# Dealing the tokens into even and odd halves in a one-core decoder trunk

## The chip, the core and the metric

The kernel runs on one core of a Trainium2 chip. The core has a matrix engine (TensorE, PE in the profile, with PEld for its weight loads), VectorE (DVE), ScalarE (ACT), GpSimd (POOL) and SyncE (SP), which work on tiles in an on-chip memory of 128 partitions (SBUF) and on accumulators (PSUM). Each engine runs its own queue in order. ScalarE and SyncE also issue DMA transfers from their queues. The metric is the device time of one execution, in microseconds.

## What is computed

A decoder trunk for 256 tokens, width 2048, in fp32. First keys and values of 256 memory tokens for both layers; then a layer of gated linear attention (GLA, 4 heads, chunks of 64 tokens), a gated feed-forward, a layer of forgetting attention (12 heads), a second feed-forward and a closing norm. Each attention layer also has 4 heads that attend to the memory. Cut to what matters:

```
mem_n = rmsnorm(mem, norm_mem)
for i in range(2):
    if i == 1:                                 # shared keys, values and forget gates
        hs = rmsnorm(x, g_kv)
        fk, fv, fl = split_cols(hs @ w_kv, [1536, 1536, 12])
        fc = cumsum(log_sigmoid(fl + b_f))     # over tokens
    mk, mv = split_cols(mem_n @ mem_w_kv[i], [512, 512])
    h = rmsnorm(x, norm_mix[i])
    if i == 0:                                 # GLA
        q, k, v, glr, og, mq = split_cols(h @ w_in, [1024, 1024, 1536, 16, 1536, 512])
        g = log_sigmoid(glr @ w_gate_up + b_gate) / 16
        # S_t = diag(exp g_t) S_{t-1} + k_t v_t^T ;  o_t = q_t S_t   (chunks of 64)
        o = headwise_rmsnorm(gla(q / 16, k, v, g)) * gn_gain * silu(og)
    else:                                      # forgetting attention, causal
        q, mq = split_cols(h @ w_in, [1536, 512])
        o = softmax(q k^T / sqrt(128) + fc[t] - fc[s]) fv
    m = softmax(mq mk^T / sqrt(128)) mv
    x = x + concat(o, m) @ w_out
    u = causal_conv3(rmsnorm(x, norm_ffn[i]) @ w_up)      # 2 x 5632 wide, over tokens
    x = x + (silu(u[:, :5632]) * u[:, 5632:]) @ w_down
return rmsnorm(x, norm_final)
```

## The kernel before

All weights are streamed from HBM in fp32, in **units** of two 128-row chunks by up to 512 columns (512 KB, tile `raw`, issued by SyncE). A panel of a projection is 8 units (16 chunks). Every weight is used in two parts: ScalarE casts the high part (`whi`, line 207), VectorE subtracts it from the weight (`wlo`, line 216), and PE does 12 matmuls of a unit: high part of the activation by high weight (228), low part of the activation by high weight (229), high part of the activation by low weight (232), for both halves of the tokens. `raw` has 4 tiles, `whi` and `wlo` 3 each, so ScalarE can be some units ahead of PE. Activations are kept as `bufA` and `bufB`, 16 tiles each of features by 256 tokens with a high and a low part (`A`, `B` in the profile); `split` (lines 343 to 347) makes the two parts, one operation on ScalarE and one on VectorE for each tile.

A panel leaves PSUM with tokens on the partitions, two accumulators of 128 tokens by 512 columns. What needs features on the partitions is turned: ScalarE scales it (`scaled`), VectorE transposes it in blocks of 32 by 32 (`square`), one DMA writes the square to DRAM and four DMAs read it back, one for each block of 128 features. These five DMAs are issued by ScalarE's queue, between the casts. The class `Turn` does this with runs of 32 tokens (128 bytes) in the reads:

```
self.rows = dp.tile([2, 4, 32, 4, 4, 32], F32, name=tag, tag=tag, bufs=bufs)
nc.scalar.dma_start(dst(k).rearrange("p (n t) -> p n t", t=32),                  # read, L301
                    self.rows[:, :, :, :, k, :].rearrange("b q i r t -> (i r) (b q) t"))
```

It serves the memory keys, the queries and keys of GLA (`qk`), the keys `fkt`, the queries and gates (`back<-turned`), and the residual `x` after each layer (`xturned`), which is split with a gain into the next projection's input (346, 347). The feed-forward has a form of its own (lines 876 to 889): it interleaves the two token halves in the square, so that its reads have 64 tokens (256 bytes) in a run. For that its scale has to be in the interleaved order too, which `mixed` makes with a product of ones and a diagonal (`row`, line 411) and two reductions (425).

Values (`mv`, `gv`, `fvt`) stay with tokens on the partitions and are only scaled (line 778 for `fvt`).

Steps that follow a panel are registered with `later((n, step), ...)` and released after the cast of the n-th unit from then on: the write at 3, the four reads at 6, and then the work on what was read, from 8 on. In GLA the gates of a head are released at 7 and its whole core, the levels of the chunked attention (lines 635 to 686), at 9. Four memory heads or four fox heads come at 8, 9, 10 and 11. The tile scheduler orders every engine's queue from a simulated timeline, in program order as the priority, with the weight loads moved up.

After the last heads comes the output projection (`add_out`), whose last two units in two panels wait for the last tiles of `mix`; after it `then` turns the new `x`, block by block, for the next projection.

Of the kernel before, what the change touches and what calls it, by code (L numbers as in the profile page):

```python
# [130 lines left out]
M_PICK = M_LVL + NVER * len(LEVELS)  # L131
M_FOX = M_PICK + 2 * T
# [4 lines left out]
def _trunk(ctx: ExitStack, tc: tile.TileContext, xt, xtok, memt, wp, wgu, gns, gfin, cnv, par, msk, out):  # L137
# [14 lines left out]
    mask = const.tile([P, M_PICK], F32, name="mask")  # L152
# [116 lines left out]
    def turned(pool, bank, width, col):  # L269

        t = pool.tile([P, T], F32, name="narrow", tag="tmp", bufs=5)
        nc.gpsimd.memset(t, 0.0)

        def take(b, a):
            S.activation(t[:, b * P : b * P + width], a, AF.Copy, scale=col[:, b : b + 1])

        def turn():
            for b in range(2):
                bs = slice(b * P, (b + 1) * P)
                TE.transpose(bank[:, bs], t[:, bs], ident)  # L280
            return bank[:, :T]

        return take, turn

    class Turn:


        def __init__(self, tag="turned", bufs=4):
            self.square = tp.tile([P, 2, 16, 32], F32, name="square", tag="square", bufs=2)
            self.rows = dp.tile([2, 4, 32, 4, 4, 32], F32, name=tag, tag=tag, bufs=bufs)  # L290

        def put(self, b, src):
            V.transpose(self.square[:, b], src.rearrange("p (c t) -> p c t", t=32))  # L293

        def write(self):
            nc.scalar.dma_start(self.rows.rearrange("b q i r k t -> (q i) b (r k t)"),
                                self.square.rearrange("p b c t -> p b (c t)"))

        def read(self, dst, blocks=range(4)):
            for k in blocks:  # L300
                nc.scalar.dma_start(dst(k).rearrange("p (n t) -> p n t", t=32),  # L301
                                    self.rows[:, :, :, :, k, :].rearrange("b q i r t -> (i r) (b q) t"))

    def back():
        return tp.tile([P, 4, T], F32, name="back", tag="back", bufs=2)

    def to_features(scales, dst, *steps):
# [3 lines left out]
        def evac(b, a):  # L311
# [12 lines left out]
            if b:  # L324
                got = []

                def read():
                    t = dst()
                    got.append(t)
                    held[0].read(t if callable(t) else lambda k: t[:, k, :])  # L330

                later((3, held[0].write), (6, read), *[(n, lambda step=step: step(got[0])) for n, step in steps])
# [3 lines left out]
    def split(dst, i, src, g=None, dealt=False):  # L336
# [12 lines left out]
    class Norm:  # L349


        def __init__(self, n, tag="x"):
            self.n, self.tag = n, tag
            self.acc = self.y = self.r = self.m = None
# [61 lines left out]

        def mixed(self, picks):

            if self.m is None:
                row = self.row()  # L420
                self.m = sm.tile([P, 2], F32, name="mixed", tag="mixed")
                for h in range(2):
                    pick = picks[:, h * T : (h + 1) * T]
                    sq = sm.tile([P, T], F32, name="sq", tag="sq", bufs=2)
                    V.tensor_tensor_reduce(sq, row, pick, 1.0, 0.0, ALU.mult, ALU.max, self.m[:, h : h + 1])  # L425
            return self.m
# [56 lines left out]
    with tc.tile_pool(name="load", bufs=1) as lp:  # L483
# [3 lines left out]
        def take_mem(g, half):  # L487
# [10 lines left out]
            for i in range(2 * half, 2 * half + 2):  # L498
                k = 4 * g + i
                split(bufA, k, mt[g][:, i, :], mraw[0][:, k : k + 1])  # L500
# [4 lines left out]
        def keys(l):  # L505
            def scaled(got):
                for f in range(MEM_H):
                    V.tensor_tensor(mk[0][:, f, :], mk[0][:, f, :], nrm.row(), ALU.mult)
# [6 lines left out]
        def mv_out(l):  # L515
            return lambda b, a: S.activation(mv[l][:, b, :], a, AF.Copy, scale=nrm.col()[:, b : b + 1])
# [13 lines left out]
        with tc.issue_after(loads[-1].ins):  # L530
# [3 lines left out]
            nc.sync.dma_start(mask[:, M_SCAN:], msk[:, M_SCAN:M_PICK])  # L534
        proj_tm(("mv", 0), bufA, mv_out(0))
        for i in range(KC):
            split(bufB, i, xf[i], gain("mix0", i))
# [10 lines left out]
    def gla(nx, then):  # L548
        h, mix = bufB, bufA
        with tc.tile_pool(name="gla", bufs=1) as gp:  # L550
# [13 lines left out]
            def first_values(b, a):  # L564
                S.activation(v0[:, b, :], a[:, :DV], AF.Copy, scale=nx.col()[:, b : b + 1])
                take(b, a[:, DV:])
# [3 lines left out]
            proj_tm(("gv", 0), h, first_values)  # L570
# [21 lines left out]
            def core(hd, q, k, v, bc):  # L592
# [41 lines left out]
                for li, B in enumerate(LEVELS):  # L634
                    H = B // 4
# [28 lines left out]
                    for i, (o, w) in enumerate(VERSIONS):  # L664
                        o4 = a3.rearrange("p b (n t) -> p b n t", t=B)[:, :, :, (i + 1) * H :]
                        for g in range(2):
# [5 lines left out]
                                              p3[gs, :, o : o + w].rearrange("p b (n t) -> p b n t", t=(3 - i) * H))  # L672
                nrm = Norm(DV, "o")
                os = []
                for j in range(3):
# [7 lines left out]
                    os.append(o)  # L683
                for j, o in enumerate(os):
# [4 lines left out]
            def take_og(j):  # L689
                def gated(c):  # L690
                    def step(g):
                        for k in (c, c + 1):
# [3 lines left out]
                            V.tensor_tensor(o, *(mix[i][:, n, :].bitcast(F32) for n in range(2)), ALU.add)  # L696
# [5 lines left out]
                proj_tm(("og", j), h, to_features([(0, 4, nx.col)], back, (8, gated(0)), (9, gated(2))))  # L702

            for hd in range(GLA_H):
                v = values(hd) if hd else v0
                if hd:
                    proj_tm(("gv", hd), h, lambda b, a: S.activation(
                        v[:, b, :], a, AF.Copy, scale=nx.col()[:, b : b + 1]))
                bc = []
                def qk():  # L710
# [5 lines left out]
                    (7, lambda t, hd=hd, bc=bc: bc.append(gates(hd))),  # L716
                    (9, lambda t, hd=hd, v=v, bc=bc: core(hd, t[:, :2, :], t[:, 2:, :], v, bc[0]))))
            for j in range(3):
# [3 lines left out]
                *[(8 + c, lambda q, c=c: mem_attention(gp, 0, q[:, c, :], c, mix)) for c in range(4)]))  # L722
# [3 lines left out]
    def fox(nx, kept, then):  # L726
        hk, hq, mix = bufB, bufA, bufB
        with tc.tile_pool(name="fox", bufs=1) as fp:
# [11 lines left out]
            def queries(f):  # L740
                got = []

                def read():
# [312 lines left out]
```

## Time and profile before

| quantity | value |
|---|---|
| time, median of 3 runs | 2272.53 us (2269.84 to 2276.99) |
| the profiled execution | 2272.12 us, span 2270.3 us |
| granted TensorE clock, mean | 0.998 |
| moved by DMA | 509.09 MB, mean 224 GB/s |
| first layer's memory and GLA stages | 0 to 430 us |
| first output projection, x turned | 430 to 515 us |
| first feed-forward | 515 to 1100 us |
| its last down projection, keys and values of fox | 1100 to 1300 us |
| fox attention, output projection, x turned | 1300 to 1550 us |
| second feed-forward | 1550 to 2200 us |
| its end, closing norm | 2200 to 2270.3 us |

A line of a timeline has the start, the duration, the engine, the source line, the operation and, in brackets, how long the engine was idle before and what released it. A line of a group ends with its busy time, the mean of one in ns, and the idle time before them. A line of waits has the engine's instruction, what it waited for, the total in us, the count and the longest.

### The profile page before, as it was taken

To read this page: it belongs to the slowest core of one execution; us is meant where nothing else is said; L and a number is where in the kernel's file an instruction comes from. 1 tells how busy PE (TensorE), PEld (TensorE's weight loads), DVE (VectorE), ACT (ScalarE), POOL (GpSimd) and SP (SyncE) were. 2 spreads that over 40 slices of the span, in tenths; PEclk is the share of its full clock that TensorE was granted. 3 is DMA by queue.
4 is the path that set the end of the run, shared out by engine and by line. 5 is a ranking of instruction groups with operands and counts; after the bars stand their busy time and mean duration, and the time that the engine had idled before them with its cause. 6 is when DMAs were issued, how large, how long until landed. Compare 5 with 4: busy or idle time off the path is not lost.

```text
span 2270.3 us, 29243 instructions
## 1 busy us (share of the span) xinstructions
PE 2246.3 (99%) x10340; PEld 1875.3 (83%) x10340; DVE 1499.7 (66%) x2329; ACT 1239.8 (55%) x1852; POOL 2.9 (0%) x15
## 2 busy tenths in 40 slices
PE   9999999999999999999999999999999999999998
PEld 7888887888888888888878898877888888888886
DVE  7568987667665577656766546656776566755766
ACT  7555565546553565445555545555655355644654
POOL 0000000000000000000000000000000000000000
PEclk9999999999999999999999999999999999999999
DMA  9765567677775777657778966677876577766774
GB/s 316 244 203 169 191 211 218 196 238 253 243 230 193 230 241 241 211 193 248 240 227 246 236 223 202 184 240 224 262 239 224 195 229 249 238 204 210 237 246 150
DMA packets 369594, 509.09 MB, mean 224 GB/s; under 512 B 245532, under 2 KB 250152, under 8 KB 369320
## 3 DMA queue, kind: packets, MB, share of 16 engines
q1 hardware_dynamic: 124584, 427.77, 56.6%
q10 hardware_dynamic: 244864, 79.46, 14.3%
q8 instruction: 81, 1.33, 0.2%
q14 instruction: 65, 0.53, 0.1%
HBM read 466.77 MB, written 40.38 MB: 223 GB/s over the span
## 4 chain that ended last, share of the span: by engine, by line
PE 89%; ACTq 3%; DMA 3%; DVE 2%; issue 1%; ACT 1%; SPq 0%; DVEq 0%
PE acc L228 29%; PE acc L232 29%; PE acc L229 29%; ACTq L301 3%; DMA xturned<-square 1%; ACT whi L207 1%; DVE wlo L216 1%; DMA turned<-square 1%; PE ps_s L659 0%; DVE B L347 0%; DVE square L293 0%; PE ps_t L454 0%; PE ps_s L461 0%; PE ps_o L472 0%; DMA mt<-memt 0%
## 5 line engine op out<-in xcount | busy, mean ns | idle before, releaser
L216 DVE TENSOR_TENSOR wlo<-raw,whi 128x1024 fp32r<-128x1024 f32 (+4 forms) x809 | 968.0, 1201 | 680.5 <-ACT whi L207 662.4
L207 ACT ACTIVATE whi<-raw 128x1024 fp32r<-128x1024 f32 (+4 forms) x809 | 840.3, 1042 | 904.6 <-PE acc L229 680.7
L228 PE MATMUL acc<-whi,B 128*128 128x512 f32 (+3 forms) x1792 | 687.3, 384 | 6.8 <-ACT whi L207 6.8
L229 PE MATMUL acc<-whi,B 128*128 128x512 f32 (+3 forms) x1792 | 684.4, 383 | 0.0
L228 PE MATMUL acc<-whi,A 128*128 128x512 f32 x1440 | 563.9, 393 | 4.1 <-ACT whi L207 3.2
L229 PE MATMUL acc<-whi,A 128*128 128x512 f32 x1440 | 561.0, 391 | 0.0
L232 PE MATMUL acc<-wlo,B 128*128 128x512 f32 (+3 forms) x1792 | 469.7, 383 | 0.0
L228 PEld LDWEIGHTS acc<-whi,B 128*128 128x128 f32 x1792 | 336.4, 188 | 70.4 <-ACT whi L207 10.0
L232 PE MATMUL acc<-wlo,A 128*128 128x512 f32 x1440 | 387.1, 390 | 0.3 <-DVE wlo L216 0.3
L229 PEld LDWEIGHTS acc<-whi,B 128*128 128x128 f32 x1792 | 336.0, 188 | 59.2
L232 PEld LDWEIGHTS acc<-wlo,B 128*128 128x128 f32 x1792 | 333.4, 188 | 60.5
L228 PEld LDWEIGHTS acc<-whi,A 128*128 128x128 f32 x1440 | 271.1, 188 | 64.3 <-ACT whi L207 6.7
L229 PEld LDWEIGHTS acc<-whi,A 128*128 128x128 f32 x1440 | 271.2, 188 | 55.8 <-DVE A L347 0.2
L232 PEld LDWEIGHTS acc<-wlo,A 128*128 128x128 f32 x1440 | 270.1, 188 | 56.9 <-DVE wlo L216 0.7
L858 ACT ACTIVATE cv<-u,cw 128x256 f32<-128x256 f32 x176 | 96.3, 588 | 11.8 <-DMA u<-turned 11.7
L859 DVE SCALAR_TENSOR_TENSOR cv<-u,cw,cv 128x256 f32<-128x256 f32 x176 | 77.7, 479 | 6.4 <-ACT cv L858 6.3
L860 DVE SCALAR_TENSOR_TENSOR cv<-u,cw,cv 128x256 f32<-128x256 f32 x176 | 77.0, 478 | 0.0
L877 DVE STREAM_TRANSPOSE square<-scaled 128x512 f32<-128x512 f32 x88 | 57.6, 690 | 0.8 <-ACT scaled L876 0.8
L876 ACT ACTIVATE scaled<-acc,mixed 128x512 f32<-128x512 f32 x88 | 55.1, 675 | 1.9 <-DVE mixed L425 1.9
L829 DVE TENSOR_TENSOR x<-x,acc 128x512 f32<-128x512 f32 x64 | 41.2, 680 | 22.4 <-PE acc L232 22.4
L438 ACT ACTIVATE sq<-x 128x256 f32<-128x256 f32 x80 | 32.4, 406 | 17.1 <-DVE x L829 16.1
L863 DVE TENSOR_TENSOR cv<-cv,cv 128x256 f32<-128x256 f32 x88 | 36.9, 419 | 1.4 <-ACT cv L862 1.4
(185 smaller groups left out, 791.0 us busy)
## 6 DMA issues: line engine op xcount, KB each, us to landing
raw<-wp SPq DMA_DIRECT2D x743, 512.0 KB, 4.2
turned<-square ACTq DMA_DIRECT2D x61, 512.0 KB, 4.4
u<-turned ACTq DMA_DIRECT2D x176, 128.0 KB, 5.2
raw<-wp SPq DMA_DIRECT2D x32, 384.0 KB, 3.1
raw<-wp SPq DMA_DIRECT2D x24, 388.0 KB, 4.2
back<-xturned ACTq DMA_DIRECT2D x64, 128.0 KB, 5.6
xturned<-square ACTq DMA_DIRECT2D x12, 512.0 KB, 4.5
back<-turned ACTq DMA_DIRECT2D x32, 128.0 KB, 4.5
```

The lines of the kernel that those rows point to most:

```text
L207: casts.append(S.activation(hi[:, s], raw[:, s], AF.Copy))
L216: V.tensor_tensor(lo[:, s], raw[:, s], hi[:, s].bitcast(F32), ALU.subtract)
L228: TE.matmul(acc[:, :n], xh, hi[:, s], start=first and j == 0, stop=False)
L229: TE.matmul(acc[:, :n], xl, hi[:, s], start=False, stop=False)
L232: TE.matmul(a, xh, ls, start=False, stop=stop)
L301: nc.scalar.dma_start(dst(k).rearrange("p (n t) -> p n t", t=32), self.rows[:, :, :, :, k, :].rearrange("b q i r t -> (i r) (b q) t"))
L829: V.tensor_tensor(x[f][:, b, :], x[f][:, b, :], a, ALU.add)
L858: S.activation(r, v[:, 2:], AF.Identity, bias=w[3], scale=w[2])
L859: V.scalar_tensor_tensor(r, v[:, 1 : T + 1], w[1], r, ALU.mult, ALU.add)
L860: V.scalar_tensor_tensor(r, v[:, :T], w[0], r, ALU.mult, ALU.add)
L876: S.activation(e, a, AF.Copy, scale=nx.mixed(picks)[:, b : b + 1])
L877: V.transpose(square[:, :, :, b], e.rearrange("p (c t) -> p c t", t=32))
```

## The change

Tokens are dealt on the host: row p of half h is token 2p + h, for `x` and for the memory; the output is put back in order. All turns then use the feed-forward's form: the square interleaves the halves, the rows in DRAM are in natural order of tokens, the write is one contiguous piece of 4 KB for each partition, and each read has runs of 256 bytes. What is read back has tokens in natural order, features on the partitions. `split` puts it back into even and odd halves as it writes the high and the low part (196 splits). The feed-forward's `mixed` and its `picks` go; it scales with the column of the norm.

The four reads go out in two pairs, at 6 and 7; the work on them comes a unit later, at 9 and on. For the residual's kept turns in fox (`queries`) the reads come at 3 + 8f and 4 + 8f. The core of a GLA head becomes a generator in six pieces, released at 9 to 14, with the gates at 8. The values, which attention needs in natural order, take a way through DRAM (`to_values`): two writes, two reads a panel, ten panels.

```
@@ class Turn
-            self.square = tp.tile([P, 2, 16, 32], F32, name="square", tag="square", bufs=2)
-            self.rows = dp.tile([2, 4, 32, 4, 4, 32], F32, name=tag, tag=tag, bufs=bufs)
+            self.square = tp.tile([P, 16, 32, 2], F32, name="square", tag="square", bufs=2)
+            self.rows = dp.tile([4, 32, 4, 4, 64], F32, name=tag, tag=tag, bufs=bufs)
...
-            V.transpose(self.square[:, b], src.rearrange("p (c t) -> p c t", t=32))
+            V.transpose(self.square[:, :, :, b], src.rearrange("p (c t) -> p c t", t=32))
...
-            nc.scalar.dma_start(self.rows.rearrange("b q i r k t -> (q i) b (r k t)"),
-                                self.square.rearrange("p b c t -> p b (c t)"))
+            nc.scalar.dma_start(self.rows.rearrange("b i r k t -> (b i) (r k t)"),
+                                self.square.rearrange("p c t h -> p (c t h)"))
...
-                nc.scalar.dma_start(dst(k).rearrange("p (n t) -> p n t", t=32),
-                                    self.rows[:, :, :, :, k, :].rearrange("b q i r t -> (i r) (b q) t"))
+                nc.scalar.dma_start(dst(k).rearrange("p (b t) -> p b t", b=4),
+                                    self.rows[:, :, :, k, :].rearrange("b i r t -> (i r) b t"))
+    def natural(v):
+        return v.rearrange("p (t h) -> p t h", h=2)
+    def halved(v):
+        return v.rearrange("p (h t) -> p t h", h=2)
+    def transfers(turn, dst, *steps):
...
+        later((3, turn.write), (6, lambda: read((0, 1))), (7, lambda: read((2, 3))),
+              *[(n, lambda step=step: step(got[0])) for n, step in steps])
+    def to_values(norm, width, dst, more=None):
+        d = dp.tile([P, 2, width], F32, name="values", tag="values", bufs=4)
...
+            e = tp.tile([P, 512], F32, name="scaled", tag="scaled", bufs=2)
+            S.activation(e[:, :width], a[:, :width], AF.Copy, scale=norm.col()[:, b : b + 1])
...
+            def write():
+                for h in range(2):
+                    nc.scalar.dma_start(d[:, h, :], held[h][:, :width])
+            def read():
+                for c in range(2):
+                    nc.scalar.dma_start(dst(c), d[64 * c : 64 * (c + 1)].rearrange("p h n -> (p h) n"))
+            later((3, write), (6, read))
@@ split
-            hi, lo, src = (t.rearrange(r, h=2) for t, r in
-                           ((hi, "p (h t) -> p h t"), (lo, "p (h t) -> p h t"), (src, "p (t h) -> p h t")))
+            hi, lo, src = halved(hi), halved(lo), natural(src)
@@ gla, a core in pieces and its release
+                    yield                  # before each of the three levels, before the norm, before the gains
...
-                    (7, lambda t, hd=hd, bc=bc: bc.append(gates(hd))),
-                    (9, lambda t, hd=hd, v=v, bc=bc: core(hd, t[:, :2, :], t[:, 2:, :], v, bc[0]))))
+                    (8, lambda t, hd=hd, v=v, go=go: go.append(core(hd, t[:, :2, :], t[:, 2:, :], v, gates(hd)))),
+                    *[(9 + i, lambda t, go=go: next(go[0], None)) for i in range(6)]))
...
-                            V.tensor_tensor(o, *(mix[i][:, n, :].bitcast(F32) for n in range(2)), ALU.add)
+                            V.tensor_tensor(natural(o), *(halved(mix[i][:, n, :].bitcast(F32)) for n in range(2)), ALU.add)
...
-                *[(8 + c, lambda q, c=c: mem_attention(gp, 0, q[:, c, :], c, mix)) for c in range(4)]))
+                *[(9 + c, lambda q, c=c: mem_attention(gp, 0, q[:, c, :], c, mix)) for c in range(4)]))
@@ ffn
-                    S.activation(e, a, AF.Copy, scale=nx.mixed(picks)[:, b : b + 1])
+                    S.activation(e, a, AF.Copy, scale=nx.col()[:, b : b + 1])
@@ preparing (the residual)
-            later((3, turns[f].write), (6, read), (8, lambda: halves(0)), (9, lambda: halves(2)))
+            transfers(turns[f], back, (9, halves(0)), (10, halves(2)))
```

What the order of instructions says of it, at three places. The line numbers of the changed kernel differ: the cast is line 206, the write 301, the read 306, `split` 378 to 382.

First ScalarE's queue after the last down projection of the first feed-forward, where the first two blocks of `x` are turned. `xturned<-square` is a write, `back<-xturned` the reads, `whi<-raw` a cast. Before:

```order
L207 ACTIVATE whi<-raw 128x1024
L296 DMA xturned<-square 128x2x512
L207 ACTIVATE whi<-raw 128x1024
L301 DMA back<-xturned 128x8x32 x4
L207 ACTIVATE whi<-raw 128x1024
L301 DMA back<-xturned 128x8x32 x4
L207 ACTIVATE whi<-raw 128x1024
L346 ACTIVATE B_100<-back,gains 128x256
```

And in the changed kernel:

```order
L206 ACTIVATE whi<-raw 128x1024
L301 DMA xturned<-square 128x1024
L206 ACTIVATE whi<-raw 128x1024
L306 DMA back<-xturned 128x4x64 x2
L206 ACTIVATE whi<-raw 128x1024
L306 DMA back<-xturned 128x4x64 x4
L206 ACTIVATE whi<-raw 128x1024
L306 DMA back<-xturned 128x4x64 x2
L206 ACTIVATE whi<-raw 128x1024
L381 ACTIVATE B_100<-back,gains 128x128x2
```

The eight reads of two blocks stood between three casts as four and four; they now stand between four casts as two, four and two, and the first split comes one cast later.

Then VectorE at the end of the GLA stage, where the last head's output (`onorm`) is split into `A_93` to `A_95`, the tiles 9 to 11 of `mix`, then added up again (`o`), multiplied with the gate (`back`) and split once more for the output projection. `mn` belongs to the first memory head. Before:

```order
L686 SCALAR_TENSOR_TENSOR onorm<-onorm,part,row 128x256 x3
L216 TENSOR_TENSOR wlo<-raw,whi 128x1024
L344 TENSOR_TENSOR A_93<-onorm,A_93 128x256
L344 TENSOR_TENSOR A_94<-onorm,A_94 128x256
L344 TENSOR_TENSOR A_95<-onorm,A_95 128x256
L696 TENSOR_TENSOR o<-A_93 128x256
L696 TENSOR_TENSOR o<-A_94 128x256
L216 TENSOR_TENSOR wlo<-raw,whi 128x1024
L696 TENSOR_TENSOR o<-A_95 128x256
L697 TENSOR_TENSOR back<-back,o 128x256 x3
L216 TENSOR_TENSOR wlo<-raw,whi 128x1024
L344 TENSOR_TENSOR A_93<-back,A_93 128x256
```

Changed:

```order
L712 SCALAR_TENSOR_TENSOR onorm<-onorm,part,row 128x256 x3
L215 TENSOR_TENSOR wlo<-raw,whi 128x1024
L379 TENSOR_TENSOR A_93<-onorm,A_93 128x128x2
L379 TENSOR_TENSOR A_94<-onorm,A_94 128x128x2
L379 TENSOR_TENSOR A_95<-onorm,A_95 128x128x2
L487 TENSOR_REDUCE mn<-ps_s 128x1 x2
L722 TENSOR_TENSOR o<-A_93 128x256
L722 TENSOR_TENSOR o<-A_94 128x256
L722 TENSOR_TENSOR o<-A_95 128x256
L723 TENSOR_TENSOR back<-back,o 128x256 x3
L215 TENSOR_TENSOR wlo<-raw,whi 128x1024
L379 TENSOR_TENSOR A_93<-back,A_93 128x128x2
```

The chain has the same links; each split now writes pairs (128x128x2), one weight subtraction fewer stands in between, and the memory head's minimum has moved ahead of the adds.

Third, ScalarE at the first panel of fox's values, with the forget gates' columns in `narrow`. Before:

```order
L207 ACTIVATE whi<-raw 128x776
L778 ACTIVATE fvt<-acc,ny 128x376
L275 ACTIVATE narrow<-acc,ny 128x12
L778 ACTIVATE fvt<-acc,ny 128x376
L275 ACTIVATE narrow<-acc,ny 128x12
L207 ACTIVATE whi<-raw 128x776
L301 DMA back<-xturned 128x8x32 x3
```

Changed:

```order
L306 DMA back<-xturned 128x4x64
L353 ACTIVATE scaled<-acc,ny 128x376
L274 ACTIVATE narrow<-acc,ny 128x12
L353 ACTIVATE scaled<-acc,ny 128x376
L274 ACTIVATE narrow<-acc,ny 128x12
L306 DMA back<-xturned 128x4x64
L362 DMA values<-scaled 128x376
L206 ACTIVATE whi<-raw 128x776
L362 DMA values<-scaled 128x376
L306 DMA back<-xturned 128x4x64 x2
L206 ACTIVATE whi<-raw 128x776
```

The scaled values go to `scaled` in place of `fvt`, and their two writes stand in the queue among the residual's reads.

More of the change, by code (lines that the diff above doesn't have):

```diff
@@ L415, in row @@
             return self.r
[L417 to L426, printed above, removed]
     class StreamNorm(Norm):
@@ L741, in queries, with read @@
                 got = []
-                def read():
-                    got.append(back())
-                    kept[f].read(lambda k: got[0][:, k, :])
+                def read(blocks):
+                    if not got:
+                        got.append(back())
+                    kept[f].read(lambda k: got[0][:, k, :], blocks)
                 def halves(c):
@@ L870, in evac @@
                     if not held:
[L871 to L874 removed]
+                        held.append(Turn("turned"))
                     e = tp.tile([P, 512], F32, name="scaled", tag="scaled", bufs=2)
[L876 to L877 removed]
+                    S.activation(e, a, AF.Copy, scale=nx.col()[:, b : b + 1])
+                    held[0].put(b, e)
                     if not b:
@@ L917, in then, with step @@
                 return
-            got = []
-            def read():
-                got.append(back())
-                turns[f].read(lambda k: got[0][:, k, :])
             def halves(c):
-                for k in (c, c + 1):
-                    split(dst, 4 * f + k, got[0][:, k, :], gain(name, 4 * f + k), dealt)
-            later((3, turns[f].write), (6, read), (8, lambda: halves(0)), (9, lambda: halves(2)))
+                def step(t):
+                    for k in (c, c + 1):
+                        split(dst, 4 * f + k, t[:, k, :], gain(name, 4 * f + k))
+                return step
+            transfers(turns[f], back, (9, halves(0)), (10, halves(2)))
         return n, then, turns
-    n, then, _ = preparing("ffn0", bufB, True)
+    n, then, _ = preparing("ffn0", bufB)
     gla(nx, then)
```

111 lines of the change are left out of this document (52 added, 59 removed).

## The prediction

> **What bounds the kernel now.** I began with the engine totals of the page, then cut TensorE's busy time (PE) into stages with the windows view, because a total says nothing about where the idle time is.
>
> ```profile
> PE 2246.3 (99%) x10340; PEld 1875.3 (83%) x10340; DVE 1499.7 (66%) x2329; ACT 1239.8 (55%) x1852; POOL 2.9 (0%) x15
> ```
>
> ```profile
> 30.00:350.00 320.00, 319.72 (x1736) 1.00 0.66 210
> 350.00:430.00 80.00, 77.81 (x353) 1.00 0.63 192
> 430.00:515.00 85.00, 83.51 (x364) 1.00 0.81 241
> 515.00:1100.00 585.00, 585.00 (x2582) 1.00 0.71 229
> 1100.00:1210.00 110.00, 106.78 (x463) 0.98 0.76 233
> 1210.00:1300.00 90.00, 87.72 (x428) 1.00 0.92 242
> 1300.00:1460.00 160.00, 160.00 (x790) 1.00 0.68 208
> 1460.00:1550.00 90.00, 86.47 (x392) 1.00 0.72 221
> 1550.00:2200.00 650.00, 650.00 (x2869) 1.00 0.72 229
> 2200.00:2270.30 70.30, 61.03 (x269) 0.95 0.52 172
> ```
>
> The columns are stretch, its length, PE's busy time, granted clock, DMA share and GB/s. PE is the bound: it is idle for 2270.3 - 2246.3 = 24.0 us of the span. Both feed-forward bodies (515 to 1100, 1550 to 2200) have no idle time, and the last row's 9.3 us is the closing norm and the store, which the change leaves as it is. That leaves about 13 us in five middle stretches: 2.2, 1.5, 3.2, 2.3 and 3.5. So a gain can only come out of those, or out of matmuls that go or run faster. The waits of PE name who ends its idle time.
>
> ```profile
> PE acc L228 <- ACT whi L207: 10.0, 10, 2.3
> PE ps_t L379 <- DVE ssq L372: 1.0, 1, 1.0
> PE ps_s L461 <- DMA back<-turned: 0.8, 1, 0.8
> PE acc L228 <- ACT A L343: 0.5, 1, 0.5
> ```
>
> Ten of the waits, 10.0 us, are for the cast of a weight unit (`whi`) on ScalarE. ScalarE is 55% busy, so it isn't short of time; something holds its queue. Its timeline in the stretch with 3.2 us idle shows what, with the queue's own DMA issues as ACTq:
>
> ```profile
> 1163.66 0.37 ACTq L296 DMA_DIRECT2D xturned<-square  x1
> 1164.18 1.06 ACT L207 ACTIVATE whi<-raw 128x1024 fp32r<-128x1024 f32 x1 [0.30 <-PE acc L229]
> 1164.19 6.87 ACTq L301 DMA_DIRECT2D back<-xturned  x4
> 1171.10 1.06 ACT L207 ACTIVATE whi<-raw 128x1024 fp32r<-128x1024 f32 x1 [5.86 <-DMA back<-xturned]
> 1171.18 5.82 ACTq L301 DMA_DIRECT2D back<-xturned  x4
> 1177.11 1.06 ACT L207 ACTIVATE whi<-raw 128x1024 fp32r<-128x1024 f32 x1 [4.94 <-issue]
> ```
>
> Four reads take 6.87 us, the next four 5.82 us, to issue, and the casts behind them stand 5.86 and 4.94 us. PE uses a unit in 12 matmuls, one every 0.23 us (rows below), or 2.7 us; three cast tiles are held, so a lone block of 4 to 5 us is about absorbed and two in a row are not. The feed-forward's reads of the same size, which already have 256-byte runs, look like this:
>
> ```profile
> 569.06 2.31 ACTq L889 DMA_DIRECT2D u<-turned  x4
> 571.50 1.06 ACT L207 ACTIVATE whi<-raw 128x1024 fp32r<-128x1024 f32 x1 [1.88 <-PE acc L229]
> ```
>
> Four take 2.31 us, and the cast after them waits for PE, not for the queue. Over all issues (min/median/max in ns, first and last start):
>
> ```profile
> L301 ACTq DMA_DIRECT2D back<-xturned x64: 366/630/4731, 433.1 to 1556.4; - x64
> L889 ACTq DMA_DIRECT2D u<-turned x176: 366/529/1695, 521.6 to 2204.4; - x176
> ```
>
> The least is 366 ns in both; it is the tail that differs, 4731 against 1695. What the change does to these reads is therefore the first term.
>
> **The change part by part.**
>
> *Reads with 256-byte runs, two and two.* All 132 reads of line 301 take the form of line 889, and the ones that go to `back`, the keys and `qk` go out as two at the sixth unit and two at the seventh. If they behave as line 889 does, the longest block in front of a cast is about 2.3 us, under one unit of PE, and the feed-forward's 0.00 us idle over 1235 us says what PE makes of that. So the waits for `whi` go: 1.5 (430 to 515), 3.2 (1100 to 1210), 3.5 (1460 to 1550), and in the key stage these:
>
> ```profile
> PE acc L228 <- ACT whi L207: 1.9, 2, 1.6
> ```
>
> That is 10.1 us. The longest stall also costs clock. Around it PE shows:
>
> ```profile
> 1173.73 0.39 PE L229 MATMUL acc<-whi,A 128*128 128x512 f32 x1
> 1173.96 0.39 PE L228 MATMUL acc<-whi,A 128*128 128x512 f32 x1
> ...
> 1178.22 0.79 PE L228 MATMUL acc<-whi,A 128*128 128x512 f32 x1 [2.29 <-ACT whi L207]
> ...
> 1180.94 0.63 PE L228 MATMUL acc<-whi,A 128*128 128x512 f32 x1
> 1181.37 0.44 PE L229 MATMUL acc<-whi,A 128*128 128x512 f32 x1
> ```
>
> Starts are 0.23 us apart before and 0.43 after it, for eight matmuls: 8 x 0.2 = 1.6 us more (the 0.98 of that stretch's clock). It goes with the stall. By the Trainium skill ("TensorE: Matmul & The Clock Gate", Part 1) the clock halves after an idle window of about 3.4 us; by that rule a stall of 2.29 us alone need not have done it, and this term would be 0. The trace shows it happening, so I keep 1.6. The wait for a read of `back` ahead of the memory scores, 0.8 us, is a landing wait of the same reads; I take it as gone too. What is left: in the two x stages two blocks' reads still fall on neighbouring units (order of the instructions), so I leave +1.0 us of waits there, between 0 and half of 10.1. Together -10.1 - 1.6 - 0.8 + 1.0 = -11.5 us.
>
> *The mixed norm of the feed-forwards.* With dealt tokens the column form of the norm fits, so a row product (line 411) and two reductions go from each feed-forward.
>
> ```profile
> 376.83 0.59 PE L411 MATMUL ps_t<-dg,mask 128*128 128x256 f32 x2
> 377.08 0.58 PE L229 MATMUL acc<-whi,A 128*128 128x512 f32 x1
> ```
>
> Such a product holds PE for 377.08 - 376.83 = 0.25 us; two of them, -0.5 us. The reductions on VectorE (DVE) and the `picks` load are hidden behind the same matmuls.
>
> *Values through DRAM.* Ten value panels now take two writes and two reads each, 40 issues more on ScalarE's queue. At the least 0.37 us each a panel's four cost 1.5 us of ScalarE spread over three units (8.2 us of PE), beside an engine 45% free; the cover is the three held casts. Without it, at the median of 0.53 to 0.63, each pair would put 1.3 us ahead of a cast, still under a unit. I take 0, with 0 to 2 us for the last key and value stretch, whose DMA share of 0.92 is the highest of the rows above. The values are first needed a panel later, so the two landings are covered.
>
> *Attention core in six pieces, steps a unit later.* The same matmuls in nearly the same order; it is the steps' release that moves. Where a panel's last step feeds the output projection, the cover is thin: the last gated block and the last heads.
>
> ```profile
> 381.47 4.01 ACTq L301 DMA_DIRECT2D back<-turned  x4
> 386.56 1.01 ACT L343 ACTIVATE A<-back 128x256 fp32r<-128x256 f32 x3
> ```
>
> One unit later is at most 2.7 us at each of the two output projections (2 x 2.7 = 5.4), and may be nothing, since the 4.01 us of issue ahead of the last splits shrinks by some 1.7. I take 0.7 and 0.3, together +1.0.
>
> *Splits that deal.* 196 splits now write neighbouring tokens into the two halves, so each written element lies 512 bytes from the last; the 12 adds of the old value to the gate read two halves. No row of before writes so. Three rows bound it. A transpose that writes every second element, and one that writes without gaps:
>
> ```profile
> L877 DVE STREAM_TRANSPOSE square<-scaled 128x512 f32<-128x512 f32 x88 | 57.6, 690 | 0.8 <-ACT scaled L876 0.8
> L293 DVE STREAM_TRANSPOSE square<-scaled 128x512 f32<-128x512 f32 x34 | 22.6, 692 | 0.0
> ```
>
> 690 and 692 ns: no cost. An elementwise operation on whole rows, and the same on every fourth element of level 4:
>
> ```profile
> L645 DVE TENSOR_TENSOR gdd<-gdd,qk 128x128 f32<-128x128 f32 x1 | 0.3, 285 | 0.0
> L645 DVE TENSOR_TENSOR gdd<-gdd,qk 128x128 f32<-128x128 f32 x1 | 0.4, 391 | 0.0
> ```
>
> 106 ns for 128 elements, 0.83 ns each: 0.21 us for a split of 256. A predicated copy in the two layouts:
>
> ```profile
> L671 DVE COPY_PREDICATED att<-mask,ps_s 64x32 f32<-64x32 int32 x2 | 0.4, 194 | 0.1
> L671 DVE COPY_PREDICATED att<-mask,ps_s 64x32 f32<-64x32 int32 x2 | 0.6, 298 | 0.1
> ```
>
> 104 ns for 32 elements, 3.3 ns each: 0.85 us for a split. A split is elementwise with two operands, so I take line 645, 0.21 us. In the feed-forwards 88 of them add 18 us to DVE over 1235 us in which it is a third idle: free. In the GLA stage nine ops of a head's tail (three splits, three adds, three splits) add 9 x 0.21 = 1.9 us to the chain that ends at the row of 386.56 above; part of it is in the 0.7 there, and up to 1.9 belongs to the range.
>
> The Trainium skill ("SBUF — State Buffer", Door 1) has a rule against this layout: SBUF is read in 16-byte lines, at least two accesses must fall in a line for full bandwidth, and every crossing pays. By it the dealt splits cost something and the alternate transposes nothing; line 645's rise agrees, but no run here shows a price for writing.
>
> Sum: 2272.12 - 11.5 - 0.5 + 0 + 1.0 = 2261.1, against the profiled execution's own time (span 2270.3 and 1.8 around it), which lies 0.4 us under the median of the runs shown, 2272.53.
>
> **The rivals.** *A, slower: the dealing fills DVE ahead of the output projection.* At 0.85 us an op the GLA stage has no room:
>
> ```profile
> 150.00:290.00 140.00, 122.30 (x273) 1.00 0.61 192
> 290.00:350.00 60.00, 55.74 (x129) 1.00 0.64 200
> ```
>
> DVE is 87% and 93% busy there. Some ten splits and adds in the second stretch add 8.5 us to 4.3 free, so the last head starts 4 us late; its own tail has nine such ops plus ScalarE's, another 9. Then the memory heads 2, the last fox heads 3, and 1.6 us of slow clock after each of the two stalls: about 21 us. 2261 - 1 + 21 = 2281. It turns into a loss from about half of that price, 0.5 us a split, and into a measurable one at 0.8. Against it: the transposes of 690 and 692 ns show no price, and line 645, the nearest in kind, a quarter of this one. Chance 0.12.
>
> *B, no change: the blocks are not the run length's.* The 6.87 us may be a backlog of the DMA queues (the weight stream runs in all of it), and landing waits of the write. Then only the spreading helps, half of the 11.5: 2272.1 - 5.8 - 0.5 + 1.0 = 2267. For it: the least issue is 366 ns in both forms. Against: 176 reads at line 889 ran beside the same stream. Chance 0.17.
>
> *C, no change: a unit later is a unit waited*, 2.7 us and 1.6 of slow clock at each output projection: 2260 + 8.6 = 2268.7. For it: the splits feed PE at once. Chance 0.10.
>
> *D, faster still:* nothing is left of the x stages' waits, nothing is lost at the projections, and the 1.0 and 0.5 us waits of the table go too: 2261.1 - 2.0 - 1.5 = 2257.6. Chance 0.15.
>
> That the change doesn't reach what it names is a rival only for the feed-forward: its 176 reads stay as they are, so nothing is due there.
>
> **How the numbers follow.** My forecast has 0.46. About 0.3%, 6.8 us, is what a measurement of this kernel tells from no change: faster is below 2265.3, slower above 2278.9. The forecast with its unknowns (0 to 2 for the values, 0 to 5 for the splits' tail) lies under the first with nearly all its chance, D wholly: faster 0.65. B, C and the upper edge of the forecast give same 0.22; A gives most of slower, 0.13. The range runs from 2255 (D with a little more) to 2276 (C with twice the dealing cost), leaving out A.
>
> **What would show it.** Right: reads of four in about 2.3 us in the x stages, `whi` waits of PE under 2 us in all, a clock of 1.00 from 1100 to 1210, splits some 0.2 us longer on DVE, and PE idle for some 15 us (24.0 - 10.1 - 0.8 + 1.0 + 1.0). Wrong: splits some 0.8 us longer and DVE over 95% from 290 to 350 (A); blocks of 4 us and more in spite of 256-byte runs (B); new waits of PE for `A` at 350 to 430 and 1460 to 1490 (C).

## The result and the profile after

The changed kernel takes 2255.3 us (2254.47 to 2256.97, 4 runs) against 2272.26 (2269.84 to 2276.99, 4 runs): ratio 0.9924, interval 0.9907 to 0.9941. A second set gave 2254.47 (2253.78 to 2254.87, 4 runs) against 2274.34, ratio 0.9906 (0.9891 to 0.9922). The gain is 17 to 20 us where 11 were forecast. The profiled execution spans 2252.7 us, 17.6 less than before.

The engine totals and the stretches of PE, as before (stretch, length, busy, clock, DMA share, GB/s):

```profile
PE 2239.9 (99%) x10336; PEld 1874.8 (83%) x10336; DVE 1525.7 (68%) x2317; ACT 1276.5 (57%) x1850; POOL 2.9 (0%) x15
```

```profile
350.00:430.00 80.00, 78.41 (x355) 1.00 0.59 194
430.00:515.00 85.00, 85.00 (x377) 1.00 0.78 250
...
1100.00:1210.00 110.00, 110.00 (x487) 1.00 0.78 251
1210.00:1300.00 90.00, 90.00 (x458) 1.00 0.84 256
...
1460.00:1550.00 90.00, 90.00 (x408) 1.00 0.78 248
1550.00:2200.00 650.00, 650.00 (x2869) 1.00 0.72 229
2200.00:2252.70 52.70, 43.32 (x190) 0.94 0.44 149
```

Four of the five stretches with idle time have none left, the slow clock of 0.98 is gone, and what remains is 1.6 us ahead of the first output projection, 1.6 us in the first 30 us (1.7 before), 0.3 us between 30 and 350 and the 9.4 us at the end (9.3 before). The waits of PE after:

```profile
PE ps_o L172 <- DVE B L169: 1.4, 1, 1.4
PE acc L227 <- ACT A L378: 1.0, 2, 0.7
PE ps_s L485 <- DMA back<-turned: 0.4, 1, 0.4
PE acc L231 <- DVE wlo L215: 0.3, 1, 0.3
PE acc L227 <- ACT whi L206: 0.2, 1, 0.2
```

The first of these lies in the opening 30 us and is the same before (1.4). Ten waits of 10.0 us for `whi` have become one of 0.2. The waits for `ssq` (1.0) and for `fc` are gone too, the latter this one of before:

```profile
PE ps_t L773 <- DVE fc L770: 0.4, 1, 0.4
```

The one for `A` has grown from 0.5 to 1.0. ScalarE in the same x stage as in the prediction's timeline:

```profile
1160.00 1.29 ACTq L306 DMA_DIRECT2D back<-xturned  x2
1162.72 1.06 ACT L206 ACTIVATE whi<-raw 128x1024 fp32r<-128x1024 f32 x1 [1.66 <-PE acc L228]
1162.72 2.79 ACTq L306 DMA_DIRECT2D back<-xturned  x4
1165.62 1.06 ACT L206 ACTIVATE whi<-raw 128x1024 fp32r<-128x1024 f32 x1 [1.84 <-PE acc L228]
1165.64 3.94 ACTq L306 DMA_DIRECT2D back<-xturned  x2
1169.68 1.06 ACT L206 ACTIVATE whi<-raw 128x1024 fp32r<-128x1024 f32 x1 [3.00 <-PE acc L231]
```

The same eight reads that took 6.87 and 5.82 us now take 1.29, 2.79 and 3.94, and for the first two casts behind them the profile names PE, not the queue, as what they waited for (the second starts 0.11 us after the end of its reads, so queue and PE came free at nearly the same time there). The queue can still stop: the last pair takes 3.94 us, and the cast at 1169.68 follows its end. But it is one such block, and PE has no wait for `whi` in this stage: the casts held ahead cover it.

### The profile page after: what moved, and what is told of

It reads as the page before. It is cut to its first block, busy times and chain, and to the rows that moved or that the text cites. A ratio compares the mean times of both kernels' runs of the same rounds, so it can differ in the third digit from the quotient of the medians.

```text
span 2252.7 us, 29275 instructions
## 1 busy us (share of the span) xinstructions
PE 2239.9 (99%) x10336; PEld 1874.8 (83%) x10336; DVE 1525.7 (68%) x2317; ACT 1276.5 (57%) x1850; POOL 2.9 (0%) x15
## 4 chain that ended last, share of the span: by engine, by line
PE 98%; DMA 1%; DVE 1%; issue 0%; ACT 0%; SPq 0%; DVEq 0%; ACTq 0%
PE acc L227 32%; PE acc L228 32%; PE acc L231 31%; DMA raw<-wp 0%; PE ps_s L683 0%; PE ps_s L485 0%; PE ps_t L478 0%; PE ps_o L496 0%; DMA xf<-xt 0%; DVE wlo L215 0%; DMA back<-turned 0%; PE ps_s L825 0%; PE ps_o L841 0%; PE ps_o L703 0%; PE ps_s L603 0%
## 5 line engine op out<-in xcount | busy, mean ns | idle before, releaser
L882 DVE SCALAR_TENSOR_TENSOR cv<-u,cw,cv 128x256 f32<-128x256 f32 x176 | 78.2, 479 | 14.9 <-ACT cv L881 14.9
L298 DVE STREAM_TRANSPOSE square<-scaled 128x512 f32<-128x512 f32 x122 | 80.0, 691 | 0.0
L896 ACT ACTIVATE scaled<-acc,ny 128x512 f32<-128x512 f32 x88 | 54.8, 674 | 0.0
```

Of the source, the lines that this page charges most:

```text
L298: V.transpose(self.square[:, :, :, b], src.rearrange("p (c t) -> p c t", t=32))
L882: V.scalar_tensor_tensor(r, v[:, 1 : T + 1], w[1], r, ALU.mult, ALU.add)
L896: S.activation(e, a, AF.Copy, scale=nx.col()[:, b : b + 1])
```

## The experiments

Each ran beside `before`, on the same chip as it. The four questions were: which part freed the queue, what the dealing and the values' detour cost, whether a later release costs, and what it is that stops the queue.

**Run length and spreading, one at a time and both.** The order of ScalarE's queue around the x stage is that of the changed kernel in the first of these three runs; only the form of the transfers differs.

```
# short_runs, in Turn, for all but the feed-forward (the write takes its old form too, in two pieces)
-            self.rows = dp.tile([4, 32, 4, 4, 64], F32, name=tag, tag=tag, bufs=bufs)
+            self.rows = dp.tile([2, 4, 32, 4, 4, 32], F32, name=tag, tag=tag, bufs=bufs)
...
-                nc.scalar.dma_start(dst(k).rearrange("p (b t) -> p b t", b=4),
-                                    self.rows[:, :, :, k, :].rearrange("b i r t -> (i r) b t"))
+                nc.scalar.dma_start(dst(k).rearrange("p (n t) -> p n t", t=32),
+                                    self.rows[:, :, :, :, k, :].rearrange("b q i r t -> (i r) (b q) t"))
...
# four_at_once, in transfers (queries alike)
-        later((3, turn.write), (6, lambda: read((0, 1))), (7, lambda: read((2, 3))),
+        later((3, turn.write), (6, lambda: read(range(4))),
# short_four: both
```

> The changed kernel, but the turns other than the feed-forward's go through DRAM in the old form (write in two pieces of 2 KB, reads with 128-byte runs); reads still two and two, order of every queue unchanged. The pieces land in another place, so the attention's and projections' inputs are scrambled in this run. If the length of the runs frees ScalarE's queue (my theory): a block of four 128-byte reads stands again ahead of a cast in each x stage, whi waits of PE come back to 4 to 7 us, the time is 2260 to 2264. If spreading two and two is what freed it (rival B): under 1 us of whi waits, 2255 to 2257.

> The changed kernel with all four reads of a turn released at the sixth unit again (and the residual's kept turns in fox with four at 3 + 8f); 256-byte runs stay. Theory run length: four reads take 2.1 to 2.3 us, which three held casts cover; 2255 to 2257, whi waits under 1 us. Rival B, spreading: 4 us and more of whi waits come back, 2260 and over.

> Both undone: 128-byte runs (scrambled as in the run with short runs) and four reads at once. Both theories: the whi waits of before return, about 10 us plus some slow clock; 2266 to 2268, that is about 5 us under before, which is then what the norm, the core in pieces and the other releases are worth. If it is at 2272 the rest of the change is worth nothing; if at 2262 or less, neither run length nor spreading was most of the gain.

| reads | two and two | four at once |
|---|---|---|
| 256-byte runs | 2255.3 (the changed kernel) | 2256.05 |
| 128-byte runs | 2260.51 | 2278.06 |

The times are medians in us. The upper left cell is from a set of its own; the second set of the changed kernel, 2254.47, comes from a chip with the same number as the other three cells. The ratios to `before` are 0.9924 (and 0.9906), 0.9908 (0.9890 to 0.9927), 0.9929 (0.9910 to 0.9949) and 1.0006 (0.9992 to 1.0020). Either part alone brings most of the gain, and without both there is none: the two don't add, each covers for the other. Without the spreading the kernel gives up 1 to 2 us, without the long runs 5 to 6, without both 23. PE's waits for `whi` in the first two runs:

```profile
PE acc L227 <- ACT whi L206: 1.6, 4, 0.8
PE acc L227 <- ACT whi L206: 2.9, 4, 1.1
```

The first line is `short_runs`, the second `four_at_once`. Both lie between the two cases that I had set out, while the times lie in the bands for the length of the runs. My expectation for the last run, 2266 to 2268, was 10 us too low. PE's waits in it:

```profile
PE acc L227 <- ACT whi L206: 14.9, 17, 2.2
PE ps_s L494 <- DMA back<-turned: 2.4, 1, 2.4
```

That is more than the 10.0 of `before`, in 17 waits (the profiled execution, at 2282.28, is one of the longer ones). So the rest of the change (norm, values, later steps, dealing) is worth nothing in sum while the queue is blocked.

**What the values' detour costs.**

```
# direct_values: to_values without DRAM
-            e = tp.tile([P, 512], F32, name="scaled", tag="scaled", bufs=2)
-            S.activation(e[:, :width], a[:, :width], AF.Copy, scale=norm.col()[:, b : b + 1])
+            S.activation(dst(b), a[:, :width], AF.Copy, scale=norm.col()[:, b : b + 1])
...
# short_four_direct: the same in short_four
```

> The changed kernel with values scaled straight from PSUM as before, without the way through DRAM: 40 transfers fewer; the reordering of the values is left out, so attention mixes other tokens. If the detour is hidden, as I put it (0, up to 2 at the last values): 2253.5 to 2255.5. If it were on the path: 2 us less or more than that.

> The run with short runs and four at once, values again without DRAM (inputs scrambled as there, reordering of the values left out). That run came to 2278 where I had 2266 to 2268, with some 8 us more stall than before in the GLA stage. If the 40 issues of the values are what the blocked queue can't take: 2269 to 2273, and the stalls at 153, 370 and 391 us go. If the later releases or the other order are to blame: within 2 us of 2278.

In the changed kernel it is 2253.84 (2252.45 to 2255.23), ratio 0.9906 (0.9893 to 0.9920): hidden, within 1.5 us. In the blocked form it is 2275.16 (2268.82 to 2281.09), ratio 1.0001 (0.9989 to 1.0013), 2.9 us under `short_four` where 5 to 9 were expected; with runs from 2268 to 2284 in both, that difference is not settled. Of the stalls that should have gone if the values' issues made them, the one at 391 us shrinks from 2.4 to 1.0, and the one of 1.6 at 153 us stays (1.5, at 149 us); what makes that one is open.

**What the dealing costs.**

```
# no_dealing
-            hi, lo, src = halved(hi), halved(lo), natural(src)
+            hi, lo, src = natural(hi), natural(lo), natural(src)
```

> The changed kernel with splits that write contiguously: the dealing into halves is left out, so the projections see the tokens in another order. In the profile each split should lose 0.2 us on VectorE and 0.25 us on ScalarE. If the dealing is off the path: 2254.5 to 2255.5. If its 1.9 us at the end of the GLA stage and at the memory heads reach PE: 1 to 2 us less, the waits for A at 418 to 423 gone.

2254.21 (2253.36 to 2256.27), ratio 0.9902 (0.9882 to 0.9923): the dealing isn't on the path to more than about 1 us, although every split pays for it. PE's wait for `A` falls from 1.0 to 0.5 without it. Splits of the changed kernel, by group (busy, mean ns of one):

```profile
L379 DVE TENSOR_TENSOR A<-cv,A 128x256 fp32r<-128x256 f32 x44 | 27.3, 624 | 0.0
L382 DVE SCALAR_TENSOR_TENSOR A<-back,gains,A 128x256 fp32r<-128x256 f32 x32 | 19.1, 683 | 0.0
L378 ACT ACTIVATE A<-cv 128x256 fp32r<-128x256 f32 x44 | 29.6, 673 | 2.3 <-DVE cv L886 2.2
L722 DVE TENSOR_TENSOR o<-A 128x256 f32<-128x256 f32 x12 | 4.8, 424 | 0.0
```

and their counterparts of before:

```profile
L344 DVE TENSOR_TENSOR A<-cv,A 128x256 fp32r<-128x256 f32 x44 | 17.7, 404 | 0.0
L347 DVE SCALAR_TENSOR_TENSOR A<-back,gains,A 128x256 fp32r<-128x256 f32 x32 | 14.2, 478 | 3.3 <-ACT A L346 3.3
L343 ACT ACTIVATE A<-cv 128x256 fp32r<-128x256 f32 x44 | 17.9, 407 | 1.3 <-DVE cv L863 1.3
L696 DVE TENSOR_TENSOR o<-A 128x256 f32<-128x256 f32 x12 | 4.7, 415 | 0.0
```

On VectorE a split costs 205 to 220 ns more, on ScalarE 266; the add, which reads its two halves in turn and writes without gaps, costs 9 more.

**Whether a unit later costs.**

```
# steps_early, and the same kernel again beside the changed one (early_again, after_again)
-   (9, gated(0)), (10, gated(2));   9 + c (memory and fox heads);   (9, halves(0)), (10, halves(2))
+   (8, gated(0)), (9, gated(2));    8 + c;                          (8, halves(0)), (9, halves(2))
```

> The changed kernel with the work on what was read a unit earlier again (8, 9 and 8 + c in place of 9, 10 and 9 + c; the GLA gates and core stay). If a unit later costs little, as in my sum (1.0): 2254 to 2255. If a unit later is a unit waited (rival C): 2250 to 2252. If the reads at the seventh unit then land too late: new waits for back, 2257 and more.

> The changed kernel on the same chip as the two beside it: 2254 to 2257.

> The run with the steps a unit earlier, on the same chip as the changed kernel: 1 to 2.5 us under it if the earlier difference (2253.4 against 2255.3) is real, under 0.5 us if it was the chip.

The first time it came to 2253.42 (2253.20 to 2253.77). On one chip the two are 2253.97 (2253.22 to 2255.31) and 2254.47 (2253.78 to 2254.87): the same. A unit later is not a unit waited; about half a microsecond at most is in it. No run here releases the core of GLA in one piece again, so what its six pieces are worth is not shown.

**What stops the queue.** In each run I took the reads issued with less than 0.3 us between them as one burst, and the median time from its start to the end of the k-th issue:

| k-th read | 1 | 2 | 3 | 4 | 5 | 6 |
|---|---|---|---|---|---|---|
| 128-byte runs, before | 0.37 | 1.01 | 3.39 | 4.54 | 8.16 | 8.87 |
| 128-byte runs, short_four | 0.37 | 1.02 | 3.40 | 4.52 | 8.80 | 9.93 |
| 256-byte runs, the changed kernel | 0.37 | 0.93 | 1.49 | 2.06 | | |
| 256-byte runs, four_at_once | 0.37 | 0.93 | 1.49 | 2.06 | | |

The first two rows leave out the feed-forward, whose reads have long runs, and rest on 3 or 4 bursts in the last two columns. Two reads of 128-byte runs (2 x 1024 runs) pass at once, and the third stops for 2.4 us in the median (in `before` it is the first issue of over 0.8 us in 17 of the 22 bursts of four); four reads of 256-byte runs (4 x 512) pass. Both make 2048 runs, though not the same bytes (256 and 512 KB). The profile's pages count such runs as packets: `short_runs` has 67585 more packets of under 512 B than the changed kernel, and 132 reads with 512 runs more are 67584.

Long runs stop too when two blocks of four meet. In the x stage of `four_at_once`:

```profile
1159.03 2.52 ACTq L306 DMA_DIRECT2D back<-xturned  x4
1161.60 1.06 ACT L206 ACTIVATE whi<-raw 128x1024 fp32r<-128x1024 f32 x1 [1.79 <-PE acc L228]
1162.48 5.30 ACTq L306 DMA_DIRECT2D back<-xturned  x4
1167.88 2.01 ACT L206 ACTIVATE whi<-raw 128x1024 fp32r<-128x1024 f32 x2 [5.23 <-DMA back<-xturned]
```

The second four start 0.93 us after the first have been issued and take 5.30 us. So I doubled the reads with long runs everywhere:

```
# eight_reads
-        later((3, turn.write), (6, lambda: read((0, 1))), (7, lambda: read((2, 3))),
+        def twice():
+            read(range(4))
+            spare = dp.tile([4, P, T], F32, name="again", tag="again", bufs=4)
+            turn.read(lambda k: spare[k], range(4))
+
+        later((3, turn.write), (6, twice),
```

> The changed kernel with each turn but the feed-forward's and fox's kept ones read twice at the sixth unit, eight reads with 256-byte runs in one go, the second four into a scratch tensor. If a burst passes at 0.51 us a read whatever its size: eight take 4.1 us, and 2255 to 2258. If ScalarE's queue stops after some 2048 runs in flight (four reads of 256-byte runs, two of 128), my reading of the three runs before: the first four take 2.1 us, eight 5.5 to 9 us, whi waits of PE of 5 us and more, 2262 to 2275.

It took 2277.5 (2271.48 to 2279.65), ratio 1.0003 (0.9992 to 1.0014): the whole gain gone, with 256-byte runs. The median times to the k-th issue are 0.37, 0.93, 1.49, 2.08 (with the feed-forward's bursts of four) and then 3.73, 4.49, 5.59, 7.07 (16 to 22 bursts): in the median the fifth read is the first to stop. Burst by burst it is looser. Of the twelve bursts of exactly eight reads, the first issue of over 0.8 us is the third in four, the fourth in one, the fifth in four, the eighth in one, and two have none. So 2048 runs is a middle value, not a limit that every burst meets. ScalarE in its x stage, with the second four as `again`:

```profile
1170.55 2.88 ACTq L306 DMA_DIRECT2D back<-xturned  x4
1173.47 1.06 ACT L206 ACTIVATE whi<-raw 128x1024 fp32r<-128x1024 f32 x1 [1.87 <-PE acc L228]
1173.49 6.09 ACTq L306 DMA_DIRECT2D again<-xturned  x3
1179.69 1.06 ACT L206 ACTIVATE whi<-raw 128x1024 fp32r<-128x1024 f32 x1 [5.16 <-DMA again<-xturned]
```

The first four pass in 2.88 us, and the cast behind them starts 2.93 us after the one before it, little more than the 2.72 that PE takes for a unit; three more take 6.09 and hold the next cast. (The second four write to DRAM, not to SBUF, and add 15 MB of traffic, so it isn't the same in every way; the rows of `four_at_once` above, all to SBUF, stop alike.) PE then waits as it did before:

```profile
PE acc L227 <- ACT whi L206: 11.8, 9, 3.0
PE ps_s L490 <- DMA back<-turned: 2.7, 1, 2.7
```

**Spreading alone, in the kernel before.** If it is the burst that counts, the old layout with reads in pairs should do much of it.

```
# before_pairs, in to_features and preparing; in queries at 1 + 6f and 2 + 6f
-                later((3, held[0].write), (6, read), *[...])
+                later((3, held[0].write), (6, lambda: read((0, 1))), (7, lambda: read((2, 3))), *[...])
```

> The kernel before with one thing changed: its four reads of 128-byte runs are released as two at the sixth unit and two at the seventh (the residual's kept turns in fox at 1 + 6f and 2 + 6f); no dealing, no detour of the values, steps where they were. If a burst of 2048 runs is what ScalarE's queue lets pass, pairs take 1.0 us and most blocks go; what stays are the two blocks that meet in an x stage: 2258 to 2263, whi waits 1 to 4 us. If the spreading only works with long runs: 2266 and over.

2264.7 (2262.86 to 2267.77), ratio 0.9954 (0.9941 to 0.9967): 9.6 of the 19.9 us that the changed kernel gains on the same chip, between my two cases. Its `whi` waits are halved, where 1 to 4 us were expected:

```profile
PE acc L228 <- ACT whi L207: 5.3, 6, 1.5
```

and its timeline in the first x stage shows why not all went:

```profile
481.37 1.00 ACTq L301 DMA_DIRECT2D back<-xturned  x2
482.49 1.06 ACT L207 ACTIVATE whi<-raw 128x1024 fp32r<-128x1024 f32 x1 [2.28 <-DVE ny L391]
482.51 4.01 ACTq L301 DMA_DIRECT2D back<-xturned  x2
486.64 1.06 ACT L207 ACTIVATE whi<-raw 128x1024 fp32r<-128x1024 f32 x1 [3.09 <-issue]
```

The first pair passes in 1.00 us. But the cast between starts as soon as it has been issued, so the second pair starts 1.14 us after the first and meets its 2048 runs. Pairs a unit apart in the program are not 2.7 us apart on a queue that is running ahead.

## Why the prediction was right or wrong

**The cause was right, its name half so.** ScalarE's queue, stopped by reads ahead of casts, was the wait, and it went. But I forecast that the length of the runs does it and held spreading as a rival with 0.17. The 2 x 2 table shows that neither is needed if the other is there. What fits all the measurements is the count of runs in the reads issued within a short time, which each part keeps to about 2048. Rival B in my words (the stop is a backlog, not the run's length) describes the mechanism better, but it gave the wrong time: only the spreading was to help, and `four_at_once` shows long runs doing it alone.

**The step that failed is the size of the stalls, which was 6 us too small.** The sum had -10.1 - 0.8 + 1.0 + 1.0 = -8.9 us for them; by the starts of the matmuls the two profiled executions differ by 14.9 us in stalls. The time came out at the lower edge of the range, 2255, and that of the second set below it. Three things make the difference. First, the reserves: +1.0 for what is left in the x stages and +1.0 for steps a unit later. PE's waits for `whi` after are 0.2, and the early steps gain 0.5 at most. Second, two more waits went: the one for `ssq`, 1.0, which I had put into rival D, and the one for `fc`, 0.4, which no term of mine has; with the scores' wait down by 0.4 and not by 0.8, and `A` up by 0.5 (rival D had it gone), that is 0.5 net. Third, and this is an error of reading: I took each stall from idle time. PE's rows overlap, a matmul is shown 0.39 us long while the next starts 0.23 us after it, so the first 0.16 us of every stall counts as busy. The row of before just ahead of the longest stall:

```profile
1174.86 1.07 PE L232 MATMUL acc<-wlo,A 128*128 128x512 f32 x4
```

Its four matmuls end at 1175.93, so the last began at 1175.54; the next was due at 1175.77 and came at 1178.22, 2.45 us late, where its row says 2.29 idle. With the ten waits for `whi` and the handful of others that is about 2 us, by this estimate. The profile says the same in sum: idle time fell by 24.0 - 12.8 = 11.2 us, busy time by 2246.3 - 2239.9 = 6.4, of which I had 1.6 for the slow clock and 0.5 for the row product; about 2 are the hidden starts of stalls. The last 2 us show when the starts of all matmuls with weights are compared, beyond the usual 0.223 us from one to the next and without the eight slow ones. Gaps of over 0.48 us go from 15 to 3 and cost 13.5 us less, 11.6 of it shown as idle. Gaps of 0.30 to 0.48 us go from 97 to 84 and cost 1.4 us less, none of it shown as idle. The other matmuls take 0.9 us less, of which I had 0.5.

**The slow clock and the row product came as forecast.** The stretch from 1100 to 1210 stands at 1.00, and no time at half clock is left before the end of the kernel. By the Trainium skill's rule ("TensorE: Matmul & The Clock Gate", Part 1), an idle window of about 3.4 us, the term would have been 0. The trace disagrees and was the better guide: the clock was halved after 2.29 us of idle time, and taking the stall away took the slow matmuls away. Where stalls came back, so did the slow clock: in `short_four` and `eight_reads` it is granted at half, for 3.4 us or (once) 6.8, after five stalls of 1.8 to 3.0 us idle, though not after every stall of that length.

**The dealing was priced right on VectorE, partly by luck.** 0.21 us was forecast from line 645, 0.205 to 0.220 measured; not forecast was 0.27 on ScalarE. But line 645 reads every fourth element, while a split writes alternately to two places. The adds, which read two places in turn, were to cost 0.21 each as well and cost 0.009, so in these rows the price goes with the writing, which no row of before shows. Rival A fell by the splits' price, and the run without dealing shows the time the same. The Trainium skill's rule in "SBUF — State Buffer" (Door 1), that every crossing to a new 16-byte line pays, agrees with the splits; by it the add in halves should have paid too, and its row rose by 9 ns.

**The detour and the later steps** were forecast at 0 and +1.0; at most 1.5 and 0.5 are in them, with either sign. Rival C is out.

**Of the signs named beforehand**, `whi` waits under 2 us, the clock, and the splits' 0.2 us held. Blocks of 2.3 us did not hold everywhere (2.79 and 3.94 in the rows above, the latter close to the 4 us that I had named as a sign of rival B), and PE's idle was 12.8 us, not 15.

## What to carry to other kernels

On this kernel a DMA issue on a computing engine's queue had a price that depended on what had been issued just before: ask how many contiguous runs a burst holds, not only how many transfers or bytes. Longer runs and fewer transfers at once are two ways to the same end, so try the cheap one first (spreading was a few lines here and gave half), and don't add their gains. And measure a stall from start to start of the engine's instructions, since pipelined rows hide the beginning of each.

## What was not expected of the hardware

In the median, ScalarE's queue let about 2048 runs pass in a burst, whether as two reads of 1024 runs of 128 bytes (1.0 us) or four of 512 runs of 256 bytes (2.06 us), and stopped at the next read (2.4 us from the second issue to the third, 1.4 from the fourth to the fifth in bursts of more than four), with the weight stream running on SyncE's queue beside it. Single bursts stopped earlier or later. That it is a count of runs, and not of transfers or bytes, is what fits these two forms and the doubled reads; where the count is kept, how fast it runs down, and whether it changes without the weight stream, was not tried.
